# A decoder layer: the sliding-window branch's projection of half 0 by Strassen-Winograd blocks, with sums read out of open PSUM banks

## The chip, the cores and the metric

One program runs on one of the eight cores of a Trainium2 chip. The core has a matrix engine (TensorE, PE), three engines for elementwise work (VectorE or DVE, ScalarE or ACT, GpSimd or POOL), and a queue (SP) that issues the transfers between HBM and the on-chip memory SBUF. The matrix engine writes into PSUM, eight banks of 128 x 512 float32. The metric is the device time of one execution in microseconds, less being better; a kernel's time is the median of its runs.

## The reference

A layer over 2048 tokens with 1024 features, batch 1, depth 1. Two attention branches run side by side, are projected to the model width, gated, added, projected again and added to the residual:

```
proj = rms_norm(h, norm_gain) @ w_in          # 1024 -> 6400 columns, split in ten parts
o_sb = stick_breaking_attention(...)          # 8 heads of 64:  512 columns
o_sw = sliding_window_sink_attention(...)     # 16 query heads: 1024 columns
y_sb = (o_sb * silu(sb_z)) @ w_branch_sb
y_sw = (o_sw * silu(sw_z)) @ w_branch_swa     # 1024 x 1024: the product that is changed
merged = sigmoid(g_sb) * y_sb + sigmoid(g_sw) * y_sw
out = rms_norm(h + merged @ w_out, final_norm_gain)
```

All of it is float32. The kernel works with rounded operands and corrections: each matrix is split into a rounded high part `h` and the remainder `l`, and a product is the three products h h, h l and l h, so that a 128 x 128 by 128 x 512 block costs three matmuls.

## The kernel before

Tokens stand in four groups of 512. The program runs over them in two halves, `halves = ([2, 3], [0, 1])`: half 0 is groups 2 and 3, half 1 groups 0 and 1. For each half it computes the input projections, the sliding-window attention and the stick-breaking attention, with gate projections woven in to keep the matrix engine busy; intermediate results go to HBM (`ow` and `od`: outputs of the two attentions; `zw`, `zs`, `gw`, `gs`: gates that have their silu or sigmoid already). After both halves' attention comes `finish`, first for half 0, then for half 1.

`finish` for one half does three things. First the banded branch (the sliding window's): for each of eight tiles of 128 output columns `d` and both groups `g`, `project` runs 8 x 3 = 24 matmuls of 128 x 512 over the split outputs `osw[k, g]` and the split weights of tile `d` into one of six PSUM banks (tags g, z, t in turn), and DVE multiplies the bank by the gate `gw[d][g]` into `part[d, g]` (L286). Second the stick-breaking branch: 12 matmuls per tile and group over `osb`, gated and added to `part` (L296, L297), split into `merged` (L299, L300). Third the output projection with `w_out` and the norm (L336 to L357).

The right-hand operands are made by `gated`: load attention output and gate, multiply on DVE (L217), round on ACT into a buffer (L219), subtract on DVE for the remainder (L220). Those of half 0's banded branch (16 blocks, 32 buffers `ringl` in the pool of `rings`) are made while the last five gate tiles of half 1 run: the loop over `gts[rest:]` at the end makes up to four after each. A gate tile is two products of 24 matmuls (L464), each evacuated by a sigmoid on ACT (L615) and, for the silu gates, a multiply on DVE (L617) and a store to `zs`; they use the two banks of tag g, so DVE's multiply frees the bank for the product after the next. The stick-breaking operands `osb` are made in `finish`, after the third tile `d`, with load buffers of tag `a` (`AB = 6` of them).

The weights come through `weights`: load 512 KB into one of two buffers `raw`, round into `wh` and subtract into `wl` (three buffers each), on POOL in half 0's finish (L117, L123: four subtracts of 128 x 256). In half 0 the split pair is also stored to HBM (`kept`), and half 1 loads the pairs from there.

Each engine works through its own queue. PE's order is the program's; the orders of DVE, ACT, POOL and of the transfers on SP in this part are set by a scheduler at build time, which goes by its own estimate of times. `finish` opens its pool `wb` on the right-hand side of SBUF, where the pools of the gates' inputs (`x`) and of temporaries (`tmp`) are closed just before; `wb` holds `fg` (the final gain), 40 buffers `ringr`, six `a`, three `res` of 128 x 1024 and three `gt` for gates.

Of the kernel before, what the change touches and what calls it, by code (L numbers as in the profile page):

```python
# [7 lines left out]
F32 = mybir.dt.float32  # L8
F32R = mybir.dt.float32r
# [34 lines left out]
def f32(ap):  # L44
    return ap.bitcast(F32)
# [3 lines left out]
def tile_kernel(ctx, tc, x, xt, meta, metat, gain, w_in, w_sb, w_sw, w_out, sinks, fgain,  # L49
# [8 lines left out]
    def DMA(dst, src):  # L58
        nc.sync.dma_start(*(t.bitcast(F32) if t.dtype == F32R else t for t in (dst, src)))
# [34 lines left out]
    def dram(name, shape, dt=F32):  # L94
        return dp.tile(shape, dt, tag=name, name=name)
# [79 lines left out]
        DMA(raw, w[c0 // P])  # L175
        return raw

    def weights(c0, w=w_in, raw=None, split=split):

        if c0 in ready:  # L180
            return ready.pop(c0)
        n = w.shape[2]
        wh, wl = (wp.tile([P, KT, P], F32R, tag=t, name=t, bufs=3)[:, :n, :] for t in ("wh", "wl"))
        key = w.name, c0
        if key in kept:
            for t, k in zip((wh, wl), kept[key]):
# [14 lines left out]

    def rings():
        lp = cst.enter_context(tc.tile_pool(name="cl", bufs=1, side="left"))
        return lambda dt=F32R: lp.tile([P, GT], dt, tag="L", name="ringl", bufs=32)

    def gated(src, zz, k, g, ring, stg):

# [24 lines left out]
        V.tensor_tensor(l, t, f32(h), op=ALU.subtract)  # L232
        return h, l

    def finish(ringl, osw, first):
        cp = cst.enter_context(tc.tile_pool(name="wb", bufs=1, side="right"))
        banks = iter(range(1 << 30))

# [23 lines left out]
        for half, groups in enumerate(halves):  # L262
            part, merged, wo = {}, {}, {}

            def out_weights(k, ch):
                raw = small("a", AB)
                DMA(raw, w_out[0, k * P:(k + 1) * P, ch * GT:(ch + 1) * GT])
                h, l = wo[k, ch] = ringr(), ringr()
                A.copy(h, raw)
                V.tensor_tensor(l, raw, f32(h), op=ALU.subtract)  # L270

            osw2 = {}
            ws_of = {}
            order = [(d, g) for ds in ([0, 1, 2], *([d] for d in range(3, 8))) for g in groups for d in ds]
            for d, g in order:
                if d == 3 and g == groups[0]:
                    osb = {(k, g): gated(od, zs, k, g, ringr, lambda: small("a", AB)) for g in groups for k in range(4)}
                if d not in ws_of:
                    ws_of[d] = first if half == d == 0 else weights(d * P, w_sw)
                ws = ws_of[d]  # L280
                acc = bank()
                project(acc, ws, [osw[k, g] for k in range(8)])
                gt = small("gt", 3)
                DMA(gt, gw[d][g])
                part[d, g] = ringr(F32)
                V.tensor_tensor(part[d, g], acc, gt, op=ALU.mult)  # L286
# [1064 lines left out]
    for half, groups in enumerate(halves):  # L1351
# [100 lines left out]
            mid.close()  # L1452
        else:
            ringl = rings()
            osw = {}
# [64 lines left out]
```

## Time and profile before

| | |
|---|---|
| time, median of 3 runs | 2091.56 us (2090.66 to 2092.18) |
| the profiled execution | 2093.26 us, its span 2091.4 us |
| PE busy | 2076.3 us, 99% of the span |
| DVE, ACT, POOL busy | 70%, 52%, 17% |
| TensorE clock granted, mean | 0.999 |
| half 0's finish begins | 1647.60 us after the span's start |

A page of the profile gives busy time by engine, the span in forty slices, DMA queues, the chain that ended last, and groups of instructions. A row of a group reads: source line, engine, operation, output tile <- input tiles, shape and count, then busy time, mean ns of one, and the engine's idle time just before them with what ended it. A row of a timeline reads: start and duration in us, engine, line, operation, tiles, count, and in brackets idle time before it with what ended it. Matmul records overlap, as one starts before its predecessor is through; the distance between starts is what one costs.

### The profile page before, as it was taken

How to read it: one execution, taken by the hardware profiler on the slowest of the kernel's cores; microseconds unless marked ns; L12 is line 12 of the kernel's file. 1: busy time of each engine (PE TensorE's matmuls, PEld its weight loads, DVE VectorE, ACT ScalarE, POOL GpSimd, SP SyncE). 2: the span in 40 equal slices, each digit the busy share in tenths (PEclk: the TensorE clock that was granted, in tenths of full speed). 3: DMA queues.
4: the chain of work that ended last, by engine and by line, in shares of the span. 5: the costliest groups of instructions: out<-in, count | busy, mean ns of one | idle time of the engine just before them, and what ended most of it. 6: DMA issues, size and time to landing. Idle time of an engine off the chain costs nothing. (4 is left out here: it accounts for less than half of the span.)

```text
span 2091.4 us, 30949 instructions
## 1 busy us (share of the span) xinstructions
PE 2076.3 (99%) x10579; PEld 1744.8 (83%) x10579; DVE 1463.0 (70%) x2383; ACT 1091.4 (52%) x2657; POOL 345.7 (17%) x682
## 2 busy tenths in 40 slices
PE   9999999999999999999999999999999999999998
PEld 7888888888888888888888888888888888788887
DVE  7897986877687754887728788777774547464543
ACT  6677774577665335777735555655653212321121
POOL 1233444331000000233310000000000343000000
PEclk9999999999999999999999999999999999999999
DMA  9855555866377574435455344343424987568532
GB/s 338 307 195 201 188 175 179 252 199 185 91 278 298 209 247 163 159 126 177 150 171 161 120 130 129 114 129 98 121 83 165 350 318 223 182 229 305 154 100 91
DMA packets 170093, 391.46 MB, mean 187 GB/s; under 512 B 23728, under 2 KB 28208, under 8 KB 169936
## 3 DMA queue, kind: packets, MB, share of 16 engines
q1 hardware_dynamic: 169648, 389.23, 55.8%
q8 instruction: 83, 1.36, 0.3%
q14 instruction: 74, 0.61, 0.1%
q10 hardware_dynamic: 288, 0.27, 0.0%
HBM read 241.68 MB, written 145.18 MB: 185 GB/s over the span
## 5 line engine op out<-in xcount | busy, mean ns | idle before, releaser
L464 PE MATMUL ps_g<-xh,wh 128*128 128x512 f32 x1264 | 517.0, 409 | 1.1 <-DVE tmp L680 0.6
L464 PE MATMUL ps_g<-xl,wh 128*128 128x512 f32 x1264 | 495.6, 392 | 0.7 <-DVE xl L1199 0.6
L464 PE MATMUL ps_g<-xh,wl 128*128 128x512 f32 x1264 | 495.7, 392 | 0.0
L928 DVE TENSOR_TENSOR_SCAN row<-row 128x512 f32<-128x512 f32 (+4 forms) x256 | 290.1, 1134 | 116.2 <-POOL row L923 60.1
L464 PEld LDWEIGHTS ps_g<-xh,wl 128*128 128x128 f32 x1264 | 237.8, 188 | 52.7
L464 PEld LDWEIGHTS ps_g<-xh,wh 128*128 128x128 f32 x1264 | 238.5, 189 | 39.9 <-ACT xh L1198 1.4
L464 PEld LDWEIGHTS ps_g<-xl,wh 128*128 128x128 f32 x1264 | 239.2, 189 | 38.0 <-DVE xl L1199 1.8
L921 ACT ACTIVATE row<-ps_z 128x512 f32<-128x512 f32 (+4 forms) x352 | 175.1, 509 | 159.3 <-PE ps_z L918 155.0
L126 ACT ACTIVATE wth<-ps_t 128x512 fp32r<-128x512 f32 (+1 forms) x320 | 171.6, 536 | 61.4 <-PE ps_t L943 59.6
L127 DVE SCALAR_TENSOR_TENSOR wtl<-ps_t,wth 128x512 fp32r<-128x512 f32 (+1 forms) x320 | 188.7, 590 | 21.3 <-ACT wth L126 20.7
L918 PE MATMUL ps_z<-kt,q 128*128 128x512 f32 (+4 forms) x704 | 183.7, 349 | 2.0 <-ACT row L921 1.9
L943 PE MATMUL ps_t<-ident,row 128*128 128x128 f32 x1088 | 171.4, 273 | 1.0 <-DVE wtl L127 0.9
L943 PEld LDWEIGHTS ps_t<-ident,row 128*128 128x128 f32 x1088 | 134.5, 140 | 33.1 <-DVE wtl L127 1.8
L918 PEld LDWEIGHTS ps_z<-kt,q 128*128 128x128 f32 x704 | 124.4, 188 | 27.4 <-ACT row L921 5.1
L975 PE MATMUL ps_o<-wth,vc 128*128 128x512 f32 (+1 forms) x320 | 131.2, 410 | 0.0
L975 PE MATMUL ps_o<-wtl,vc 128*128 128x512 f32 (+1 forms) x320 | 116.4, 364 | 0.0
L767 ACT ACTIVATE sc<-sc,nm 128x129 f32<-128x129 f32 x256 | 100.0, 393 | 30.5 <-DVE nm L765 29.5
L934 POOL COPY mr<-row 128x16 f32<-128x16 f32 x128 | 28.4, 224 | 444.2 <-DVE row L928 401.8
L615 ACT ACTIVATE tmp<-ps_g 128x512 f32<-128x512 f32 x80 | 48.0, 600 | 80.5 <-PE ps_g L464 74.3
L299 ACT CAST ringl<-gt 128x512 fp32r<-128x512 f32 x32 | 19.9, 621 | 127.1 <-DVE gt L297 93.3
L117 POOL TENSOR_SCALAR wh<-raw 128x1024 fp32r<-128x1024 f32 (+1 forms) x45 | 49.8, 1108 | 212.7 <-PE ps_g L464 90.3
L123 POOL TENSOR_TENSOR wl<-raw,wh 128x256 fp32r<-128x256 f32 x88 | 83.2, 975 | 2.0
(442 smaller groups left out, 4202.3 us busy)
## 6 DMA issues: line engine op xcount, KB each, us to landing
wh<-h_in_w_in SPq DMA_DIRECT2D x66, 512.0 KB, 3.9
wl<-l_in_w_in SPq DMA_DIRECT2D x66, 512.0 KB, 5.1
h_in_w_in<-wh SPq DMA_DIRECT2D x50, 512.0 KB, 3.3
l_in_w_in<-wl SPq DMA_DIRECT2D x50, 512.0 KB, 4.1
raw<-in_w_in SPq DMA_DIRECT2D x49, 512.0 KB, 5.3
q<-qd SPq DMA_DIRECT2D x128, 128.0 KB, 3.2
vc<-vd SPq DMA_DIRECT2D x48, 256.0 KB, 3.2
kd<-tmp SPq DMA_DIRECT2D x32, 256.0 KB, 3.4
```

The costliest lines, as they stand in the source:

```text
L117: G.tensor_scalar(h, src, 1.0, 1.0, op0=ALU.mult, op1=ALU.mult)
L123: G.tensor_tensor(l[:, c], src[:, c], f32(h[:, c]), op=ALU.subtract)
L126: A.activation(h, acc, AF.Copy, scale=scale)
L127: V.scalar_tensor_tensor(l, acc, scale, f32(h), op0=ALU.mult, op1=ALU.subtract)
L464: T.matmul(acc, lhsT=a[:, k, :], rhs=b[:, k, :], start=k == i == 0, stop=k == KT - 1 and i == 2)
L615: A.activation(e, acc, AF.Sigmoid)
L767: A.activation(sc[:, hh, :], sc[:, hh, :], AF.Exp, bias=nm[:, hh:hh + 1], accum_out=den[:, hh:hh + 1])
L918: T.matmul(z[:, :m], lhsT=qt[:, j * P:(j + 1) * P], rhs=kt[h][:, k0 + c:k0 + c + m], start=t == 0, stop=t == 1)
L921: A.activation(r[:, c:c + m], z[:, :m], AF.Sigmoid, scale=-1.0)
L928: V.tensor_tensor_scan(r[:, :w], r[:, :w], r[:, :w], last[j] if n else 1.0, op0=ALU.mult, op1=ALU.min)
L943: T.transpose(tr[:, j * P:(j + 1) * P], rows_of[h, g, n - (j > i), j][:, k0:k0 + P], ident)
L975: T.matmul(o[:, :n], lhsT=v, rhs=r, start=first and r is wh, stop=last)
```

## The change

Half 0's banded product is done for pairs of column tiles. With the left and right operands cut in two along the inner dimension (k of 0 to 3 and 4 to 7, `HK = 4`), two tiles `d`, `d + 1` and the two groups `ga`, `gb` make a 2 x 2 by 2 x 2 block product, and seven block products of 12 matmuls take the place of eight. Four pairs make the eight tiles; `branch_by_pairs` does two pairs (`a`, `a + 1` and `b`, `b + 1`) at a time, for c = 0 and c = 4.

The right-hand blocks b11, b21, t1, b22, t2, t3, t4 (each for four k, high and low) are made by `outputs_blocks` in the gate tail for k = 0, 1, 2; for k = 3 only b11 and b21 are made there, and `last_blocks` makes the rest at the start of `finish`. `ringl` has 43 buffers instead of 32, `ringr` 29 instead of 40, and the constants' buffers `wm` and `vm`, no longer needed, serve as three more. The left-hand blocks come from `weight_blocks`, a generator of seven `wh`, `wl` tiles per c, each of two 512-column blocks: plain quarters are rounded on ACT with the subtract on POOL, the sums r1 to r4 and q1 to q4 are made on POOL (eight subtracts of 128 x 256 for each set, in buffers `a`), rounded on ACT, with the subtract on DVE. Two tiles are made ahead of `finish`; two whole quarters per c are loaded into buffers `res`.

Sums over products are formed in PSUM as far as they can be: the products for `za` (b11, then t2, then t3, then t4) go into one bank of tag o that stays open, and between them the partial sum is read: by `keep` (a copy on ACT to SBUF) or by `gated_sum` (on DVE: bank plus a kept partial sum, then times the gate). The last t4 product of each c is put off (`rest`) to after the first product that follows. `half_way`, after the b21 products of c = 4, makes the stick-breaking operands `osb` in buffers that are free by then. Half 0's weights are no longer stored; half 1 loads the plain weights again and splits them, with the rounding on ACT (`hsplit`) and the subtract on POOL.

```diff
@@ -175,7 +175,7 @@
         DMA(raw, w[c0 // P])
         return raw
 
-    def weights(c0, w=w_in, raw=None, split=split):
+    def weights(c0, w=w_in, raw=None, split=split, keep=True):
 
         if c0 in ready:
             return ready.pop(c0)
@@ -188,6 +188,8 @@
             return wh, wl
         raw = load(c0, w) if raw is None else raw
         split(wh, wl, raw)
+        if not keep:
+            return wh, wl
         kept[key] = [dram(f"{t}_{w.name}_{c0}", [P, n, P], F32R) for t in "hl"]
         for t, k in zip((wh, wl), kept[key]):
             if put_off is None:
@@ -201,7 +203,7 @@
 
     def rings():
         lp = cst.enter_context(tc.tile_pool(name="cl", bufs=1, side="left"))
-        return lambda dt=F32R: lp.tile([P, GT], dt, tag="L", name="ringl", bufs=32)
+        return lambda dt=F32R: lp.tile([P, GT], dt, tag="L", name="ringl", bufs=43)
 
     def gated(src, zz, k, g, ring, stg):
 
@@ -232,7 +234,205 @@
         V.tensor_tensor(l, t, f32(h), op=ALU.subtract)
         return h, l
 
-    def finish(ringl, osw, first):
+    def part_split(h, l, t):
+        A.copy(h, t)
+        V.tensor_tensor(l, t, f32(h), op=ALU.subtract)
+
...
+    def outputs_blocks(blk, k, ga, gb, ring, stg, zed):
+
+        def product(kk, g):
+            a, z = stg(), zed()
+            DMA(a, ow[kk][g])
+            DMA(z, zw[kk][g])
+            V.tensor_tensor(a, a, z, op=ALU.mult)
+            return a
+
+        def put(name, t):
+            h, l = blk[name, k] = ring(), ring()
+            part_split(h, l, t)
+
+        b11, b21 = product(k, ga), product(k + HK, ga)
+        put("b11", b11)
+        put("b21", b21)
+        if k == HK - 1:
+            return
+        b12, b22 = product(k, gb), product(k + HK, gb)
+        t3 = stg()
+        V.tensor_tensor(t3, b22, b12, op=ALU.subtract)
+        V.tensor_tensor(b12, b12, b11, op=ALU.subtract)
+        put("t1", b12)
+        put("b22", b22)
+        V.tensor_tensor(b22, b22, b12, op=ALU.subtract)
+        put("t2", b22)
+        put("t3", t3)
+        V.tensor_tensor(b21, b21, b22, op=ALU.subtract)
+        put("t4", b21)
+
+    def last_blocks(blk, ga, gb, ring, stg, zed):
+
+        k = HK - 1
+
...
+        for t, kk in ((b12, k), (b22, k + HK)):
+            z = zed()
+            DMA(t, ow[kk][gb])
+            DMA(z, zw[kk][gb])
+            V.tensor_tensor(t, t, z, op=ALU.mult)
+        t3, t4 = stg(), stg()
+        V.tensor_tensor(t3, b22, b12, op=ALU.subtract)
+        for part in blk["b11", k]:
+            V.tensor_tensor(b12, b12, f32(part), op=ALU.subtract)
+        put("t1", b12)
+        put("b22", b22)
+        V.tensor_tensor(b22, b22, b12, op=ALU.subtract)
+        put("t2", b22)
+        put("t3", t3)
+        for part, t in zip(blk["b21", k], (b22, None)):
+            if t is not None:
+                V.tensor_tensor(t4, f32(part), t, op=ALU.subtract)
+            else:
+                V.tensor_tensor(t4, t4, f32(part), op=ALU.add)
+        put("t4", t4)
+
+    def weight_blocks(spare_raw, sums):
+
+        def tile_of(*srcs):
+            wh, wl = (wp.tile([P, KT, P], F32R, tag=t, name=t, bufs=3) for t in ("wh", "wl"))
+            out = []
+            for i, (src, on_pool) in enumerate(srcs):
+                c = slice(i * HK, (i + 1) * HK)
+                A.copy(wh[:, c], src)
+                if on_pool:
+                    for j in range(0, HK, 2):
+                        G.tensor_tensor(wl[:, c][:, j:j + 2], src[:, j:j + 2], f32(wh[:, c][:, j:j + 2]), op=ALU.subtract)
+                else:
+                    V.tensor_tensor(wl[:, c], src, f32(wh[:, c]), op=ALU.subtract)
+                out.append((wh[:, c], wl[:, c]))
+            return out
+
+        def quarter(d):
+            raw = spare_raw()
+            DMA(raw, w_sw[d])
+            return raw[:, :HK], raw[:, HK:]
+
...
+        def combine(c, d):
+            (a11, a12), (a21, a22) = c, d
+            r1, r2, r3, r4 = (sums() for _ in range(4))
+            difference(r1, a21, a22, ALU.add)
+            difference(r2, r1, a11)
+            difference(r4, a12, r2)
+            difference(r3, a11, a21)
+            return r1, r2, r3, r4
+
+        for c in (0, 4):
+            one, two = ((raw[:, :HK], raw[:, HK:]) for raw in (load(d * P, w_sw) for d in (c, c + 2)))
+            yield tile_of((one[0], True), (two[0], True))
+            yield tile_of((one[1], True), (two[1], True))
+            low = quarter(c + 1)
+            r1, r2, r3, r4 = combine(one, low)
+            yield tile_of((r1, False), (r2, False))
+            yield tile_of((r4, False), (r3, False))
+            low2 = quarter(c + 3)
+            q1, q2, q3, q4 = combine(two, low2)
+            yield tile_of((q1, False), (low[1], True))
+            yield tile_of((q2, False), (q4, False))
+            yield tile_of((q3, False), (low2[1], True))
+
...
+        def product(acc, w, name, start=False, stop=False):
+            wh, wl = w
+            for k in range(HK):
+                h, l = blk[name, k]
+                T.matmul(acc, lhsT=wh[:, k, :], rhs=h, start=start and k == 0, stop=False, skip_group_check=True)
+                T.matmul(acc, lhsT=wh[:, k, :], rhs=l, start=False, stop=False, skip_group_check=True)
+                T.matmul(acc, lhsT=wl[:, k, :], rhs=h, start=False, stop=stop and k == HK - 1, skip_group_check=True)
+
+        def keep(d, g, acc):
+            t = part[d, g] = new()
+            A.copy(t, acc)
+
+        def gated_sum(d, g, acc):
+            t = part[d, g]
+            V.tensor_tensor(t, acc, t, op=ALU.add)
+            V.tensor_tensor(t, t, gate_of(d, g), op=ALU.mult)
+
...
+        rest = []
+        for c in (0, 4):
+            a, b = c, c + 2
+            w = fetch()
+            za = ps("o")
+            product(za, w[0], "b11", True)
+            keep(a, ga, za)
+            for f in rest:
+                f()
+            rest = []
+            zb = ps("o")
+            product(zb, w[1], "b11", True)
+            keep(b, ga, zb)
+            w = fetch()
+            for d, wi in zip((a, b), w):
+                acc = bank()
+                product(acc, wi, "b21", True, True)
+                gated_sum(d, ga, acc)
+            if c:
+                half_way()
+            w = fetch()
+            x = bank()
+            product(x, w[0], "t1", True)
+            keep(a + 1, gb, x)
+            product(za, w[1], "t2")
+            keep(a, gb, za)
+            w = fetch()
+            product(x, w[0], "b22", stop=True)
+            gated_sum(a, gb, x)
+            product(za, w[1], "t3")
+            gated_sum(a + 1, gb, za)
+            w = fetch()
+            x = bank()
+            product(x, w[0], "t1", True)
+            keep(b + 1, gb, x)
+
+            def close(d, z, w):
+                product(z, w, "t4", stop=True)
+                t = part[d, ga] = new()
+                V.tensor_tensor(t, z, gate_of(d, ga), op=ALU.mult)
+
+            close(a + 1, za, w[1])
+            w = fetch()
+            product(zb, w[0], "t2")
+            keep(b, gb, zb)
+            product(x, w[1], "b22", stop=True)
+            gated_sum(b, gb, x)
+            w = fetch()
+            product(zb, w[0], "t3")
+            gated_sum(b + 1, gb, zb)
+            rest.append(lambda d=b + 1, z=zb, w=w[1]: close(d, z, w))
+        return rest
+
+    def finish(ringl, blk, blocks, ahead, raws):
         cp = cst.enter_context(tc.tile_pool(name="wb", bufs=1, side="right"))
         banks = iter(range(1 << 30))
 
@@ -240,7 +440,7 @@
             return ps("gzt"[next(banks) % 3])
 
         def ringr(dt=F32R):
-            return cp.tile([P, GT], dt, tag="R", name="ringr", bufs=40)
+            return cp.tile([P, GT], dt, tag="R", name="ringr", bufs=29)
 
         def small(tag, bufs):
             return cp.tile([P, GT], F32, tag=tag, name=tag, bufs=bufs)
@@ -265,18 +465,43 @@
             def out_weights(k, ch):
                 raw = small("a", AB)
                 DMA(raw, w_out[0, k * P:(k + 1) * P, ch * GT:(ch + 1) * GT])
-                h, l = wo[k, ch] = ringr(), ringr()
+                if half == 0:
+                    rings_of = (ringr, ringr) if (k, ch) < (6, 1) or ch == 0 else (ringr, ringl) if k == 6 else (ringl, ringl)
+                else:
+                    rings_of = (ringl, ringl) if ch == 0 and k < 3 else (ringr, ringr)
+                h, l = wo[k, ch] = [ring() for ring in rings_of]
...
             osw2 = {}
             ws_of = {}
-            order = [(d, g) for ds in ([0, 1, 2], *([d] for d in range(3, 8))) for g in groups for d in ds]
+            rest = []
+            if half == 0:
+                osb = {}
+                spare_raw = lambda: cp.tile([P, D], F32, tag="xr", name="res", bufs=3).rearrange("p (k c) -> p k c", k=KT)
+                raws.append(spare_raw)
+                raws.append(lambda: small("a", AB).rearrange("p (k c) -> p k c", k=HK))
+
+                def gate_of(d, g):
+                    gt = small("gt", 3)
+                    DMA(gt, gw[d][g])
+                    return gt
+
+                def half_way():
+                    ring = slots([ringl() for _ in range(10)] + [ringr() for _ in range(3)] + [wm[0], wm[1], columns(vm[:, 0:2])])
+                    osb.update({(k, g): gated(od, zs, k, g, ring, lambda: small("a", AB)) for g in groups for k in range(4)})
+
+                last_blocks(blk, *groups, ringr, lambda: ringr(F32), lambda: small("a", AB))
+                rest = branch_by_pairs(groups, blk, ahead, blocks, part, bank, lambda: ringr(F32), gate_of, half_way)
+            else:
+                hsplit[0] = True
+            order = [(d, g) for ds in ([0, 1, 2], *([d] for d in range(3, 8))) for g in groups for d in ds] if half else ()
             for d, g in order:
                 if d == 3 and g == groups[0]:
-                    osb = {(k, g): gated(od, zs, k, g, ringr, lambda: small("a", AB)) for g in groups for k in range(4)}
+                    osb = {(k, g): gated(od, zs, k, g, ringl if k == 3 else ringr, lambda: small("a", AB))
+                           for g in groups for k in range(4)}
                 if d not in ws_of:
-                    ws_of[d] = first if half == d == 0 else weights(d * P, w_sw)
+                    ws_of[d] = weights(d * P, w_sw, keep=False)
                 ws = ws_of[d]
                 acc = bank()
                 project(acc, ws, [osw[k, g] for k in range(8)])
@@ -291,6 +516,9 @@
                 for g in groups:
                     acc = bank()
                     project(acc, ws, [osb[k, g] for k in range(4)])
+                    for f in rest:
+                        f()
+                    rest = []
                     gt = small("gt", 3)
                     DMA(gt, gs[d][g])
                     V.tensor_tensor(gt, acc, gt, op=ALU.mult)
@@ -1452,8 +1680,8 @@
             mid.close()
...
-            todo = [(k, g) for g in halves[0] for k in range(8)]
+            blk = {}
+            todo = list(range(HK))
...
-                for k, g in todo[:4]:
-                    osw[k, g] = gated(ow, zw, k, g, ringl, tmp)
-                del todo[:4]
-            for k, g in todo:
-                osw[k, g] = gated(ow, zw, k, g, ringl, tmp)
-    first = weights(0, w_sw)
+                for k in todo[:1]:
+                    ring = ringl if k < HK - 1 else slots([ringl(), wm[0], wm[1], columns(vm[:, 0:2])])
+                    outputs_blocks(blk, k, *halves[0], ring, tmp, ring_x)
+                del todo[:1]
+            assert not todo
+    raws = []
+    blocks = weight_blocks(lambda: raws[0](), lambda: raws[1]())
+    ahead = [next(blocks), next(blocks)]
     fst.close()
-    finish(ringl, osw, first)
+    finish(ringl, blk, blocks, ahead, raws)
     cst.close()
 
 _OUT = (2048, 1024)
```

More of the change, by code (lines that the diff above doesn't have):

```diff
@@ L233, in gated_in_place, with slots, columns @@
         return h, l
-    def finish(ringl, osw, first):
+    def part_split(h, l, t):
+        A.copy(h, t)
+        V.tensor_tensor(l, t, f32(h), op=ALU.subtract)
+    def slots(tiles):
+        it = iter(tiles)
+        return lambda: next(it)
+    def columns(t):
+        return t.rearrange("p a b c -> p (a b c)")
+    def outputs_blocks(blk, k, ga, gb, ring, stg, zed):
[24 more added lines that the diff above has]
+        put("t4", b21)
@@ new lines, in last_blocks, with put @@
+    def last_blocks(blk, ga, gb, ring, stg, zed):
+        k = HK - 1
+        def put(name, t):
+            h, l = blk[name, k] = ring(), ring()
+            part_split(h, l, t)
+        b12, b22 = stg(), stg()
+        for t, kk in ((b12, k), (b22, k + HK)):
[18 more added lines that the diff above has]
+        put("t4", t4)
@@ new lines, in weight_blocks, with difference @@
+    def weight_blocks(spare_raw, sums):
[16 more added lines that the diff above has]
+            return raw[:, :HK], raw[:, HK:]
+        def difference(t, a, b, op=ALU.subtract):
+            for j in range(0, HK, 2):
+                G.tensor_tensor(t[:, j:j + 2], a[:, j:j + 2], b[:, j:j + 2], op=op)
+            return t
+        def combine(c, d):
[19 more added lines that the diff above has]
+            yield tile_of((q3, False), (low2[1], True))
@@ new lines, in branch_by_pairs, with fetch @@
+    def branch_by_pairs(groups, blk, ahead, blocks, part, bank, new, gate_of, half_way):
+        ga, gb = groups
+        def product(acc, w, name, start=False, stop=False):
[12 more added lines that the diff above has]
+            V.tensor_tensor(t, t, gate_of(d, g), op=ALU.mult)
+        def fetch():
+            ahead.append(next(blocks, None))
+            return ahead.pop(0)
+        rest = []
[48 more added lines that the diff above has]
+        return rest
@@ L1454, in tile_kernel @@
             ringl = rings()
-            osw = {}
-            todo = [(k, g) for g in halves[0] for k in range(8)]
+            blk = {}
+            todo = list(range(HK))
             for mk in gts[rest:]:
```

## The prediction

> **What bounds the kernel now.** I read the page first, for the engine that is full; then the waits of TensorE over the last 590 us, where the change lies; then busy time by stretches of 50 us around half 0's finish; then the timelines of the engines and of the DMA queue from 1604 to 1706 us.
>
> ```profile
> span 2091.4 us, 30949 instructions
> PE 2076.3 (99%) x10579; PEld 1744.8 (83%) x10579; DVE 1463.0 (70%) x2383; ACT 1091.4 (52%) x2657; POOL 345.7 (17%) x682
> PE   9999999999999999999999999999999999999998
> ...
> PE ps_z L337 <- DVE ringr L270: 0.5, 2, 0.2
> ```
>
> The last line is the only wait of TensorE after 1500 us: 0.5 us in all. So every matmul taken out is worth its issue time, and every wait put in is paid in full: there is no slack on PE to hide it in.
>
> ```profile
> core 0: us, PE busy (x) PEld busy (x) DVE busy (x) ACT busy (x) POOL busy (x), PEclk, DMA share, GB/s
> ...
> 1600.00:1650.00 50.00, 50.00 (x222) 41.41 (x221) 27.96 (x38) 13.50 (x23) 12.26 (x12) 1.00 0.87 308
> 1650.00:1700.00 50.00, 50.00 (x223) 41.38 (x222) 24.38 (x30) 6.76 (x10) 22.31 (x24) 1.00 1.00 377
> 1700.00:1750.00 50.00, 50.00 (x222) 41.42 (x221) 24.04 (x32) 6.44 (x11) 16.47 (x20) 1.00 0.66 214
> ...
> 1647.60 0.39 PE L258 MATMUL ps_g<-ringl,wh 128*128 128x512 f32 x1
> 1653.04 0.39 PE L258 MATMUL ps_z<-ringl,wh 128*128 128x512 f32 x1
> ```
>
> Half 0's finish starts at 1647.60, called T0 below. From its first matmul to the next product's are 24 matmuls in 5.44 us, so one costs 0.2267 us of PE, not the 0.39 us of its own row, which overlaps its neighbours. The DMA engines are full (share 1.00, 377 GB/s) just there, while the vector engines are about half idle.
>
> **What the change removes.** The banded product of half 0 was 8 tiles x 2 groups x 24 = 384 matmuls; now it is 4 pairs x 7 products x 12 = 336. The program as built has 48 matmuls fewer on PE. 48 x 0.2267 = **-10.9 us**. Also gone are the 8 x 2 stores of split weights, 512 KB each, and half 1 loads 8 x 512 KB instead of 16 x 512 KB. That relieves a DMA system which PE does not wait for, so I cost it at nothing, as I do half 1's new splits: one cast and four POOL subtracts (4.5 us at most, rows below) per tile of 10.9 us of PE, with three buffers. If that cover went, PE would wait up to 3 us there.
>
> **What it adds and where it lies.** The sums of the right-hand blocks and of the weight quarters are new work for DVE, ACT and POOL, and its prices are in these rows:
>
> ```profile
> 1661.63 0.69 DVE L286 TENSOR_TENSOR ringr<-ps_g,gt 128x512 f32<-128x512 f32 x1 [8.28 <-DMA gt<-gw]
> 1662.24 0.68 DVE L286 TENSOR_TENSOR ringr<-ps_z,gt 128x512 f32<-128x512 f32 x1
> ...
> 1681.05 2.31 DVE L220 TENSOR_TENSOR ringr<-a,ringr 128x512 fp32r<-128x512 f32 x2
> 1683.28 1.22 DVE L217 TENSOR_TENSOR a<-a 128x512 f32<-128x512 f32 x1
> 1684.43 2.37 DVE L220 TENSOR_TENSOR ringr<-a,ringr 128x512 fp32r<-128x512 f32 x2
> ...
> 1670.53 2.83 POOL L123 TENSOR_TENSOR wl<-raw,wh 128x256 fp32r<-128x256 f32 x4
> 1681.76 4.49 POOL L123 TENSOR_TENSOR wl<-raw,wh 128x256 fp32r<-128x256 f32 x4
> L219 ACT CAST ringl<-tmp 128x512 fp32r<-128x512 f32 x16 | 9.9, 622 | 28.2 <-DVE tmp L217 28.1
> ```
>
> A 128x512 DVE operation costs 0.61 us of its queue alone (start to start, first two rows), and a 128x256 POOL subtract 2.83/4 = 0.71 us. Where POOL subtracts and DVE's SBUF-to-SBUF operations run together (1681 to 1686) both slow down: DVE five in 5.75 us, 1.15 us each, POOL 4.49/4 = 1.12 us. A cast on ACT is 0.62 us.
>
> Order matters as much as price. The engines take their queues in order:
>
> ```profile
> 1650.94 0.62 ACT L219 CAST ringl<-tmp 128x512 fp32r<-128x512 f32 x1 [2.58 <-DVE tmp L217]
> 1651.46 0.59 ACT L615 ACTIVATE tmp<-ps_g 128x512 f32<-128x512 f32 x1
> 1652.67 0.68 DVE L617 TENSOR_TENSOR tmp<-ps_g,tmp 128x512 f32<-128x512 f32 x1
> ```
>
> The sigmoid L615 reads the last gate product, ended by about T0+0.2; it ran 3.7 us later, behind a cast that stood waiting for DVE. Before, this hurt nobody. In the program as built, the copies `keep` (PSUM to SBUF, without which the next product may not go into the open bank) stand in the same ACT queue:
>
> ```
> ACT: cast wh<-r1, cast t1h, ... cast wh<-q1, cast t4h, keep(za), keep(zb), keep(x), ...
> ACT, second half: ... cast of gated output 7 of 8, keep(x), keep(za), ...
> ```
>
> (the gated outputs are the stick-breaking ones, which `half_way` queues). Terms in order of time, all waits of PE:
>
> **Gate tail: +1.5 (0 to 4).** DVE has 57 operations instead of 40 in the last four gate tiles (49 for the blocks, 8 silu products that release PE's two `ps_g` banks): 57 x 0.61 = 35 us of 43.5, with POOL beside 8 of them. Before, the L617 at 1652.67 came 5 us after its product; one product lasts 5.44 us, so there was hardly margin, and some of it goes.
>
> **t1 waits for its weights: +6 (4 to 9).** Buffers of the finish lie where the gates' inputs and temporaries were, so its loads cannot start before the gates end:
>
> ```profile
> 1653.37 0.32 SPq L59 DMA_DIRECT2D zs<-tmp  x1
> ...
> 1655.57 0.33 SPq L59 DMA_DIRECT2D fg<-in_fgain  x1
> 1655.96 1.53 SPq L59 DMA_DIRECT2D gt<-gw  x3
> ...
> raw<-in_w_sw SPq DMA_DIRECT2D x8, 512.0 KB, 6.4
> gt<-gs SPq DMA_DIRECT2D x32, 256.0 KB, 3.1
> ```
>
> fg goes 2.2 us after the last gate's store; the first gt, issued 0.4 us later, is used at 1661.63, 5.7 us after issue. Before, nothing urgent hung on that (a drained bank is needed 10.9 us later at the earliest, three rotate). Now the last store goes at about T0+1.8 (product drained 0.2, sigmoid 0.59, multiply 0.68, handing on), fg at 4.0, then at 0.4 us each two pairs for `last_blocks`, landing from 10.6, and the first quarter of weights, issued at 6.1, landing 6.4 later at 12.5. Two POOL sums (1.4 to 2.2) and a cast give r1 at 14.6 to 15.4, its low part 1.15 us later. PE reaches t1 after 48 matmuls, at 10.9. That is 4 to 6 us late; if the gate tail ends as late as before, 4 us more.
>
> **t2 waits for keep(za): +11.5 (3 to 13).** keep(za) stands behind the cast of t4h, which ends `last_blocks`. DVE's queue from its first product to that point holds 17 operations (12 of `last_blocks`, 5 low parts of weights), all SBUF to SBUF, and POOL has some 16 subtracts in the same stretch: 17 x 1.15 = 19.6 from 10.6, so 30.2, with two casts 31.5. t2 could start at 10.9+6+2.7 = 19.6. At 0.61 us each, 22.3. I take the crowded price, since POOL has no pause there.
>
> **Rest of the first four columns: +2 (0 to 3)**, for low parts a POOL operation late.
>
> **b22 of the second half waits for keep(x): +12 (8 to 19).** That copy stands behind the seventh of eight gated outputs. Their 24 loads share six `a` buffers, also used by the weight sums; the second to seventh find room only when the third tile of the second half is split, after product 15: 15 x 2.72 + 19.5 = T0+60.3. Before, the eight took
>
> ```profile
> 1664.19 0.69 DVE L213 TENSOR_TENSOR a<-a 128x512 f32<-128x512 f32 x1 [1.27 <-DMA a<-od]
> ...
> 1704.31 1.16 DVE L220 TENSOR_TENSOR ringr<-a,ringr 128x512 fp32r<-128x512 f32 x1 [0.69 <-ACT ringr L219]
> ```
>
> 41.3 us, 5.2 each, with DMA full. With 3.1 to 5.2 us for a landing (rows above) and 2.7 us of arithmetic, two in flight, one takes 3 to 4; I take 4: 60.3+24 = 84.3, plus the copy, 85. PE stands there at 73.9. At 3.5 the wait is 8, at 5.2 it is 19. Behind it POOL's remaining sums are late too: **+2.5 (0 to 4)**.
>
> **The clock: +3.5 (0 to 5).**
>
> ```profile
> 10.00:12.00 2.00, 1.86 (x5) 1.48 (x6) 2.00 (x5) 1.92 (x3) 0.00 (x0) 0.60 1.07 357
> 12.00:14.00 2.00, 2.00 (x7) 1.57 (x6) 1.90 (x4) 1.15 (x3) 0.00 (x0) 0.55 1.17 286
> ...
> 10.14 0.59 PE L464 MATMUL ps_g<-xl,wh 128*128 128x512 f32 x1 [0.62 <-DVE xl L1199]
> 10.53 0.63 PE L464 MATMUL ps_g<-xh,wh 128*128 128x512 f32 x1
> ...
> 13.89 0.39 PE L464 MATMUL ps_g<-xl,wh 128*128 128x512 f32 x1
> ```
>
> At the start, after a wait of 0.6 us, the granted clock was 0.60 and 0.55 for nearly 4 us: nine matmuls, from 10.14 to 13.89, took 3.75 us, not 9 x 0.2267 = 2.04, and 1.7 us were lost. Of the three long waits the first's slow stretch falls into the second wait; two count, 3.5 us. The Trainium skill ("TensorE: Matmul & The Clock Gate", Part 1) speaks against this change here: an idle window of about 3.4 us halves the clock until a busy window has passed; without that rule nothing in this trace says that a wait in mid-kernel is followed by slow matmuls, and the sum would be 3.5 us lower.
>
> The skill's page "SBUF — State Buffer" (Who interferes with whom) calls the port that VectorE and GpSimd share an exclusive lock. The rows say otherwise in size: a pair takes about 1.14 us, less than 0.61 + 0.71 = 1.32. By a full lock the 17 operations would take 22.4 us and the sum would be 2.8 us higher.
>
> **Sum.** 1.5 + 6 + 11.5 + 2 + 12 + 2.5 + 3.5 = 39 us of waits, less 10.9: +28.1. The profiled execution took 2093.26 us (span 2091.4), 1.7 above the median; it becomes 2121.4, and the median of 2091.56 becomes **2119.7 us**. 0.2%, 4.2 us, is about what a measurement of this kernel can tell from no change.
>
> **Rivals.**
> *The gain stands (faster).* If loads land in 3.1 us instead of 5.7 to 6.4 and POOL and DVE do not slow each other, t1's wait is 1 to 2, t2's 3 or less, and the outputs are done before b22. It decides where all waits stay under 6.7 us: then 2081 to 2087. For it: 12 MB less DMA traffic. Against: the contended rows and the queue order, which no faster load changes. 4%, and 3% for a tie near 2092.
> *Only the first half stalls.* If the outputs run at 3 us each or are loaded sooner, terms 12, 2.5 and one clock loss go: +28.1 - 16.3 = +12, 2104. 10%.
> *The outputs go at the old pace and the gate tail is late.* 3 + 9 + 13 + 3 + 19 + 4 + 5 - 10.9 = +45, 2137. For it: 5.2 us each is what was measured; against: the stores that filled the DMA are gone. 11%.
> That the matmuls are not saved is excluded by the program.
>
> **Numbers.** The forecast has 72%. Below 2104 lie the first rival, the tie and half of the second (12%), above 2134 most of the third (8 to 10%). Slower 93%, same 3%, faster 4%.
>
> **Right or wrong.** PE would show waits for ACT at the matmuls of `product` (t1: 4 to 7 us; t2: about 11, on the copy of `ps_o`; one of about 12 in the second half, on the copy of `ps_g`), ACT idle behind DVE ahead of the t4h cast, POOL subtracts near 1.1 us, and PEclk under 1 between T0 and T0+110. Wrong would be: no such waits, copies that run ahead of the casts, or half 1's finish changed by more than 3 us.

## The result, and the profile after

The changed kernel takes **2118.6 us** (median of 4 runs, 2117.56 to 2121.04), the kernel before 2091.87 beside it (4 runs, 2090.66 to 2092.55): ratio **1.0133**, 95% interval 1.0121 to 1.0144, 26.7 us slower. The forecast was 2119.7, slower. The profiled execution of after took 2121.04 us.

The head of its page:

```profile
span 2119.3 us, 31014 instructions
PE 2072.7 (98%) x10531; PEld 1738.3 (82%) x10531; DVE 1503.4 (71%) x2441; ACT 1126.0 (53%) x2717; POOL 392.1 (19%) x730
...
PE   9999999999999999999999999999999779999998
```

PE has 10531 instructions where it had 10579: the 48 matmuls are gone. In exchange two slices fall to 7 where PE had 9 throughout. The waits of TensorE after 1500 us (in total, times, longest):

```profile
PE ps_g L365 <- ACT ringr L371: 11.6, 1, 11.6
PE ps_o L365 <- ACT ringr L371: 9.0, 1, 9.0
PE ps_t L365 <- ACT wh L315: 5.1, 1, 5.1
PE ps_t L564 <- ACT ringr L473: 2.9, 1, 2.9
PE ps_g L692 <- DVE tmp L845: 1.9, 1, 1.9
PE ps_o L365 <- DVE ringr L421: 0.8, 1, 0.8
PE ps_o L365 <- DVE ringr L375: 0.7, 1, 0.7
```

In order of time these are the gate tail (1.9), t1 (5.1), t2 (9.0), the drain of `ps_o` between the halves (0.8), b22 of the second half (11.6), a late sum (0.7) and half 0's output projection (2.9). Before, there were 0.5 us of such waits. The timelines of VectorE, ScalarE and TensorE around the three long ones:

```profile
1663.41 0.62 ACT L315 CAST wh<-a 128x512 fp32r<-128x512 f32 x1 [13.34 <-POOL a L331]
1664.08 0.79 PE L365 MATMUL ps_t<-ringl,wh 128*128 128x512 f32 x1 [5.12 <-ACT wh L315]
...
1676.56 1.21 DVE L305 TENSOR_TENSOR ringr<-ringr,vm 128x512 f32<-128x512 f32 x1
1677.80 0.62 ACT L238 CAST ringr<-ringr 128x512 fp32r<-128x512 f32 x1 [5.22 <-DVE ringr L305]
1678.32 1.07 ACT L371 COPY ringr<-ps_o 128x512 f32<-128x512 f32 x2
1678.95 0.79 PE L365 MATMUL ps_o<-ringl,wh 128*128 128x512 f32 x1 [8.97 <-ACT ringr L371]
...
1733.77 0.62 ACT L221 CAST ringr<-a 128x512 fp32r<-128x512 f32 x1 [2.08 <-DVE a L219]
1734.29 0.58 ACT L371 COPY ringr<-ps_g 128x512 f32<-128x512 f32 x1
1734.93 0.80 PE L365 MATMUL ps_g<-ringl,wh 128*128 128x512 f32 x1 [11.65 <-ACT ringr L371]
```

T0 is the first matmul of half 0's finish, 1647.92 here. ACT stands still for the addition that ends the arithmetic of t4 in `last_blocks` (L305), casts t4h (the high part of t4), then copies the bank whose product ended at T0+2.7, and t2 starts 0.6 us later. In the second half the copy follows a gated output's cast (L221) in the same way. After each long wait the clock is low, by the windows (behind POOL's column stand PEclk, DMA share and GB/s):

```profile
1664.00:1668.00 4.00, 3.87 (x8) 2.67 (x9) 3.94 (x4) 1.59 (x4) 4.00 (x5) 0.50 0.11 43
1679.00:1683.00 4.00, 4.00 (x10) 3.13 (x11) 3.55 (x5) 0.87 (x2) 4.00 (x5) 0.50 0.15 21
1683.00:1687.00 4.00, 4.00 (x18) 3.31 (x17) 1.81 (x3) 1.63 (x3) 3.37 (x6) 0.93 0.69 245
1733.00:1737.00 4.00, 2.07 (x5) 1.69 (x6) 3.84 (x5) 2.21 (x4) 3.91 (x4) 0.50 0.34 88
```

After t1's and t2's waits eight to ten matmuls start in 4 us, where 18 fit; b22 begins in the middle of the last window, five matmuls in 2 us. From T0 to the end of the span after takes 471.4 us, before took 443.8 (2091.4 less 1647.60). This stretch leaves out what varies between executions upstream and is used below.

### The profile page after: what moved, and what is told of

It is laid out like the page before. It is cut to its first block, busy times and chain, and to the rows that moved or that the text cites. A ratio compares the mean times of both kernels' runs of the same rounds, so it can differ in the third digit from the quotient of the medians.

```text
span 2119.3 us, 31014 instructions
## 1 busy us (share of the span) xinstructions
PE 2072.7 (98%) x10531; PEld 1738.3 (82%) x10531; DVE 1503.4 (71%) x2441; ACT 1126.0 (53%) x2717; POOL 392.1 (19%) x730
## 5 line engine op out<-in xcount | busy, mean ns | idle before, releaser
L1027 POOL TENSOR_SCALAR_AFFINE_SELECT pm<-ph 64x256 fp32r<-64x256 f32 x128 | 63.3, 495 | 113.4 <-ACT ph L126 109.2
L576 ACT ACTIVATE sq<-res 128x512 bf16<-128x512 f32 (+1 forms) x33 | 20.4, 618 | 117.9 <-DVE res L568 117.8
```

## The experiments

Theory 1 is the prediction's reading: the order of ScalarE's queue holds the copies back. Theory 2, formed on the trace of after: DVE and POOL have more work between T0+10 and t4 than time, and while both subtract in SBUF each is slow, so whatever is moved ahead makes something else late. All times are medians.

### 1. The copies first

```
 product(zb, w[1], "b11", True); keep(b, ga, zb)
+if not c:
+    last_blocks(...)                # was ahead of the branch
+    ahead.append(next(blocks))      # the first sums: were ahead of za
```

> Edit: the last row of right-hand blocks (last_blocks) and the first sums are queued behind the first two keep copies, so keep(za) stands behind nothing of last_blocks; no work is added or taken out. Theory 1, the order of ScalarE's queue (the prediction's step): t2's wait of 9.0 us, with its 2.3 us of slow clock, goes; 2107 to 2110 us. Theory 2, the amount of work: the blocks and weights of the first half need some 17 VectorE operations at 1.15 us beside GpSimd's sums from about 10 us after the start of half 0's finish, in whatever order; the copy runs early, TensorE waits for last_blocks' blocks inside t1 instead (about 8 us, at its fourth row of blocks), and more for the b22 and later products; 2117 to 2121 us.

**2120.51 us**, ratio to before 1.0141 (1.0126 to 1.0156): nothing won. Its waits:

```profile
PE ps_g L365 <- ACT ringr L371: 11.6, 1, 11.6
PE ps_t L365 <- ACT ringr L238: 6.5, 1, 6.5
PE ps_t L365 <- ACT wh L315: 2.8, 1, 2.8
PE ps_t L365 <- ACT ringr L371: 2.8, 1, 2.8
...
PE ps_t L366 <- DVE ringr L239: 0.8, 1, 0.8
```

The copy now runs at T0+4.1, and t2 does not wait. In its place t1 waits for its fourth row of blocks (the cast L238: 6.5, and 0.8 for the low part), and b22 waits 2.8 for the copy of `x`, which stands behind the same t4h cast. Theory 1 as the prediction put it falls: the copy was only the last thing late. VectorE's timeline shows the rest:

```profile
1667.42 1.21 DVE L320 TENSOR_TENSOR wl<-a,wh 128x512 fp32r<-128x512 f32 x1
1668.55 1.21 DVE L295 TENSOR_TENSOR ringr<-ringr,wm 128x512 f32<-128x512 f32 x1
1669.68 1.21 DVE L320 TENSOR_TENSOR wl<-a,wh 128x512 fp32r<-128x512 f32 x1
1670.82 2.34 DVE L239 TENSOR_TENSOR ringr<-ringr 128x512 fp32r<-128x512 f32 x2
```

Every operation is at the crowded price, and the planner of the queues, which orders all but TensorE's by its own estimate, has put five low parts of weights (L320), most of them for later products, ahead of t1's low part (L239 at 1670.82). So this run moved more than the copies, and does not by itself tell work from order.

### 2. The weight quarters first

```
-DMA(fg, fgain...)                      # ahead of last_blocks' loads
+for d in (1, 3): DMA(spare_raw(), w_sw[d])
 ...
+DMA(fg, fgain...)                      # behind the branch
```

> Edit: the loads of the first two weight quarters go ahead of the load of fg and of last_blocks' loads (fg's load is moved behind the banded branch); no work is added or taken out. The prediction's step: t1 waits because its quarter is asked for at 6.1 to 7.6 us after the start of half 0's finish; asked for at 4, t1's wait of 5.1 us falls to 1 to 2 and the time by 3 to 4, 2114 to 2116 us, with the wait at t2 as it was. Rival, the amount of work: GpSimd's sums start 4 us sooner and so run beside more of last_blocks' work on VectorE, t1 starts sooner but waits some 8 us at its fourth row of blocks, and t2 8 us; the time stays at 2117 to 2120 us.

**2120.03 us**, ratio 1.0138 (1.0123 to 1.0154). The rival holds:

```profile
PE ps_g L368 <- ACT ringr L374: 11.2, 1, 11.2
PE ps_t L368 <- ACT ringr L238: 7.8, 1, 7.8
PE ps_o L368 <- ACT ringr L374: 7.4, 1, 7.4
```

t1's wait for weights is gone (0.3 left), and 7.8 us stand at its fourth row of blocks. The late load was the last cause of the 5.1 us and not the only one.

### 3. Without `last_blocks`

```
-last_blocks(...)
+for name in ("t1", "b22", "t2", "t3", "t4"): blk[name, 3] = blk[name, 2]
```

> Left out: the arithmetic and the loads of last_blocks; the products of row 3 take row 2's blocks instead. TensorE's work is the same. Theory 1 (queue order) and theory 2 (amount of work) both have t2's wait of 9.0 us gone and t1's down to 3 to 4, with 12 VectorE operations fewer beside GpSimd's sums: 2105 to 2109 us. Rival, late weights alone: t2 would wait for GpSimd's sums in any case (r2's and r4's splits), and the time would fall by under 4 us, 2115 to 2118. The second half's wait at b22 stays at 11 to 14 us in all.

**2103.39 us**, ratio 1.0057 (1.0040 to 1.0074): 15.2 less than after, somewhat more than expected. t2's wait is gone, t1's is 1.7, b22's is 11.4, as in after. Weights alone would have let t2 start in time.

### 4. Without the sums

```
-r1..r4 = sums of quarters on GpSimd
+return a21, a22, a11, a12
```

> Left out: the eight sums of weight quarters of each pair (GpSimd's L331 operations, 48 in all); raw quarters are split in their place, as many splits as before, and six buffers are free of sums. Theory 2 (amount of work at the port that VectorE and GpSimd share, and a buffers held by sums): last_blocks' operations run at 0.6 to 0.7 us instead of 1.15, t2's wait falls from 9.0 to 6 to 7, and the second half's gated outputs find free buffers at once, so that the wait at b22 falls from 11.7 to 1 to 3 us; 2099 to 2105 us. Theory 1 (order on ScalarE alone, outputs at 4 us each whatever the buffers): the wait at b22 stays at 9 to 12 and the time falls by 3 to 6 us, 2112 to 2116.

**2101.94 us**, ratio 1.0051 (1.0036 to 1.0066): 16.7 less than after.

```profile
PE ps_o L360 <- ACT ringr L366: 6.7, 1, 6.7
PE ps_t L360 <- ACT wh L315: 3.6, 1, 3.6
```

t2's wait is 6.7 as expected, and b22's 11.6 us are gone altogether, though the eight gated outputs are as many: the first of them begins at 1668.3 instead of 1693.6, since its loads find `a` buffers. The crowding goes with the sums too, but it is not what slowed the outputs in after, where GpSimd works 2.1 us between 1704 and 1733. There the second half's first four sums hold four of the six buffers. One load of an output goes out at 1698.24, the next only once the first low part made from a sum is through:

```profile
1709.23 1.28 DVE L320 TENSOR_TENSOR wl<-a,wh 128x512 fp32r<-128x512 f32 x2
1709.93 0.32 SPq L59 DMA_DIRECT2D a<-od  x1
```

So the outputs are late by the sums' buffers, as the prediction's step at b22 had it. They need not be the only cause: the queue stood 4.2 us for a gate's buffer (released by L421) just before it waited for L320. This run has 32 GpSimd instructions fewer than after (698 against 730), not the 48 that the expectation names.

### 5. All queues by hand

The same products, but every queue of the branch in the order of need:

```
+with tc.manual_schedule(engines={DVE, Activation, Pool, SP}):
+    quarter 1; b12, b22; quarter 3; gates    # loads
+    r1, r2 -> cast, low; t1; b22; t2; r4; r3; t3; q1; q2; t4; q4; q3
+    # sums of columns 0 to 3 on V, of 4 to 7 on G; keep before casts that wait
+    # gated outputs: two loaded in the first half, then one between products
+output weights' second half loaded ahead of half 1's raw weights; gt 3 -> 4 buffers
```

The low parts of four plain quarters, on GpSimd in after, are on VectorE too, here and in experiments 6 and 9.

> The same seven products, same arithmetic, with the order of all queues of half 0's banded branch written out by hand: the weight sums of columns 0 to 3 on VectorE instead of GpSimd (those of columns 4 to 7 stay on GpSimd, early), each sum, block and low part queued in the order in which TensorE needs it, each keep copy ahead of casts that wait, quarters loaded first, the gated outputs spread over the second half; the second column half of the output weights is loaded ahead of half 1's weights; four gt buffers instead of three (one ringr fewer). Theory 2 (amount of work at the shared port, and when it starts): VectorE alone needs 18 operations of 0.61 us for what t1 to t3 wait for, 11 us, where the crowded pairs took 17 x 1.15 us, so the waits of 5.1, 9.0 and 11.7 us shrink to 2 to 3 in the first half and 2 to 4 in the second, the wait of 2.9 at the output projection and the slow clock go: 2079 to 2086 us, faster than before. Rival: reading partial sums out of open banks, with a copy or an add between two products of a bank, costs its wait in any order; then 2092 or more.

**2087.43 us** (11 runs) against 2090.9 of before (27): ratio **0.9984**, interval 0.9975 to 0.9993, the fastest of all. It is 3.5 us under before and about 31 under after. It misses the expected range (2079 to 2086) by 1.4 us; the rival, 2092 or more, is 4.6 off. Page and waits:

```profile
span 2084.9 us, 30994 instructions
PE 2067.0 (99%) x10531; PEld 1735.0 (83%) x10531; DVE 1505.9 (72%) x2453; ACT 1126.4 (54%) x2717; POOL 374.4 (18%) x706
```
```profile
PE ps_g L1037 <- DVE tmp L1190: 1.8, 1, 1.8
PE ps_z L447 <- ACT ringr L453: 0.9, 1, 0.9
PE ps_g L807 <- ACT wm L539: 0.8, 1, 0.8
PE ps_g L808 <- DVE vm L540: 0.6, 1, 0.6
PE ps_t L448 <- DVE ringr L507: 0.2, 1, 0.2
```

As many matmuls as after, VectorE as busy as after (1505.9 against 1503.4), and 2.5 us of waits behind T0 instead of 30. So neither the open banks nor the amount of vector work as such costs the time. From T0 (1648.97) to the end it takes 435.9, which is 7.9 less than before: 10.9 less the waits, within 1 us. Between the two profiled executions that leaves 6.6 us (2093.26 less 2086.66), since T0 is 1.4 later, by the gate tail's wait of 1.8, which was left alone. The medians lie closer, 3.5: the profiled execution of before was 2.4 above the median here, that of this kernel 0.8 below its own.

### 6. By hand, with the sums on GpSimd

```
-r1 = a21 + a22 ...  (VectorE, columns 0 to 3, all eight sums)
+the same on GpSimd, two operations each
```

> As e5_by_hand, but the weight sums of columns 0 to 3 are on GpSimd, as in the kernel after; the order is otherwise the same. Theory 2: VectorE's operations beside them take 1.15 instead of 0.61 us again, and t1, t2 and b22 wait 8 to 9 us in all instead of 3: 4 to 7 us slower than e5_by_hand. Rival, only the order of the queues mattered: within 1.5 us of e5_by_hand.

**2092.41 us**, ratio 1.0009 (0.9999 to 1.0018): 5.0 above experiment 5, as theory 2 has it. VectorE's timeline there with GpSimd's beside it, then VectorE's in experiment 5 for the same work:

```profile
1659.11 1.21 DVE L496 TENSOR_TENSOR wl<-a,wh 128x512 fp32r<-128x512 f32 x1
1660.25 1.22 DVE L581 TENSOR_TENSOR a<-ringr,ringl 128x512 f32<-128x512 f32 x1
1659.74 2.32 POOL L484 TENSOR_TENSOR a<-raw,a 128x256 f32<-128x256 f32 x2
```
```profile
1659.82 0.68 DVE L496 TENSOR_TENSOR wl<-a,wh 128x512 fp32r<-128x512 f32 x1
1660.42 0.68 DVE L581 TENSOR_TENSOR a<-ringr,ringl 128x512 f32<-128x512 f32 x1
```

1.14 us from start to start beside GpSimd, 0.60 without. But this kernel has the sums of after on the engine of after, and is 26 us faster than after, of which 6.7 belong to the stage behind the branch (experiment 9). So theory 2 is wrong where it says "in whatever order": by these differences the order is worth some 19 us and the crowding 5, only it is the order of all queues, with early loads, and not that of two copies. The 19 include the four low parts that stay on VectorE here; what they give was not tried apart.

### 7. The waits filled

```
+fill(20)   # ahead of t1      fill(46) ahead of t2      fill(48) ahead of b22
```

> The kernel after, with matmuls that nobody reads put into the three long waits: 20 before t1, 46 before t2, 48 before b22 of the second half (into a free PSUM bank, from blocks that lie in SBUF anyway), 0.2267 us each, so 4.5, 10.4 and 10.9 us: TensorE is not idle for long. Theory: the idle time halves the granted clock, so t2's and b22's products run at 0.2267 us a matmul again, the clock before t2 makes no difference in time, and 2.3 + 1.6 us come back: 2113 to 2116 us. Rival: the low clock comes of something else (a cap on power, the copies): no change, 2117 to 2121; if the added matmuls delay the product behind them, up to 2 us slower.

**2119.57 us**, ratio 1.0139 (1.0125 to 1.0152): no gain in the median, where 2113 to 2116 was expected. Once more, beside after on the same chip:

> e7_filled_waits once more, beside the kernel after on the same chip (e11_after_again), to tell 2 us apart. Theory: the clock's two stretches cost 2.3 and 1.6 us, of which 1.5 come back as a longer wait behind b22, as the traces of e7_filled_waits and of after have it: 1.5 to 2.5 us under e11_after_again. Rival: none of it is left in the total, within 1 us.

> The kernel after, unchanged, for e10_filled_waits_again to stand against: 2117 to 2120 us by every theory.

Filled **2120.61** (2119.99 to 2121.26), after **2119.73** (2118.89 to 2120.23). The filled kernel's windows (the second run):

```profile
1679.00:1683.00 4.00, 3.56 (x15) 2.92 (x16) 4.00 (x5) 1.98 (x5) 4.00 (x5) 1.00 0.18 60
1733.00:1737.00 4.00, 3.94 (x17) 3.30 (x18) 4.00 (x5) 2.33 (x5) 4.00 (x4) 1.00 0.13 25
```

The clock stays at 1.00 where after has 0.50, so idle time is what lowers it. And from T0 to the end the filled kernel takes 469.5 and 469.6 us in its two profiles, after 471.4 and 471.6: in this stretch 2 us come back, as the second expectation had it, where the first had 3.9 (a wait for a sum behind b22, 0.5 to 0.7 us in after, is 2.2 here). The totals do not show it: T0 lies later in the second pair of profiles (1648.73 against 1646.86), not in the first (1647.52 against 1647.92). Where the total loses what the stretch wins stays open.

### 8. Half 1's part alone

```
 # in the kernel before
-store split weights in half 0, load them in half 1
+keep=False: half 1 loads raw weights and splits them, cast on ScalarE
```

> The kernel before with only the weights' part of the change: the split banded weights are not stored in half 0, and half 1 loads and splits them again (its cast on ScalarE, as after). The prediction's step put this at nothing, up to 3 us: 2091 to 2093. Against it, after waits 2.9 us at half 0's output projection for output weights whose loads stand on the DMA queue behind a load of half 1's raw weights: 2094 to 2097, with that wait in the trace.

**2093.26 us** (10 runs), ratio 1.0012 (1.0003 to 1.0021): 2.4 slower. The DMA queue's timeline, then the wait:

```profile
1783.01 0.33 SPq L59 DMA_DIRECT2D raw<-in_w_sw  x1
1783.39 7.41 SPq L59 DMA_DIRECT2D a<-in_w_out  x8
```
```profile
PE ps_z L340 <- ACT ringr L271: 2.0, 1, 2.0
```

The output weights' loads go out directly behind a load of half 1's raw weights on the same queue; after them ScalarE waits 5.3 us for the first to land. Counted from each kernel's T0 they go out 2.7 us later than in before (137.9 against 135.2). The median lies between the two expected ranges; the wait is there, 2.0 of the 2.9. No gain from the stores that are gone shows in the total.

### 9. Only the branch by hand

```
 # experiment 5 without its last line: gt 3 buffers, loads ordered as in after
```

> As e5_by_hand, but only the banded branch is ordered by hand: three gt buffers, 29 ringr, and the order of the output weights and of half 1's loads as in the kernel after. Theory 2 with the finding of e8_half1_alone: the branch itself waits as little as in e5_by_hand (4 to 5 us), but VectorE comes out of it behind, and with three gt buffers (each held for about 4 us of work and 4 of loading while a product lasts 2.72) it cannot catch up before half 0's output projection, where TensorE then waits for the last merged tiles and the output weights, 6 to 10 us: 2092 to 2097 us. Rival, the branch's order was all that mattered: within 3 us of e5_by_hand, 2086 to 2090.

**2094.16 us** (10 runs), ratio 1.0009 (1.0000 to 1.0018): 6.7 above experiment 5, or 6.2 when each is set against before as measured beside it (2091.39 here, 2090.9 there).

```profile
PE ps_g L905 <- DVE ringl L867: 2.4, 2, 2.1
...
PE ps_g L903 <- ACT ringl L866: 1.3, 1, 1.3
```

These two, 3.7 us, stand at the start of half 0's output projection, for the last merged tiles, and are less than the 6 to 10 us expected. The eight matmuls behind them, at a granted clock of 0.55 to 0.59, took another 1.7 us more than at full speed. The branch itself waits as in experiment 5, within 1 us. So what was done in the branch (its order, and the sums' engine) is worth 24 us of the 31, and the rest lies in the stage behind it, 40 us later. How much of that the fourth gt buffer gives and how much the order of the loads was not tried apart.

## Why the prediction was right

- **48 matmuls, -10.9:** held. Experiment 5 has the same 48 fewer and keeps 7.9 of it behind T0.
- **Gate tail, +1.5:** 1.9 in this profile, 0.9 in after's second one, 0.2 in experiment 1's. Held, in a size that varies.
- **t1, +6:** 5.1, for r1's cast behind POOL, as said; fg went at T0+4.05 (forecast 4.0). The size held. That the load is the cause held in part: with the load early (experiment 2) a wait of 7.8 stands at t1's fourth row instead.
- **t2, +11.5:** 9.0, and 2.4 us of slow matmuls in t1 that this wait would else have held: 11.4. VectorE does have 17 operations up to the cast of t4h, and they take 20.0 us (1657.80 to 1677.77, forecast 19.6). But the crowded price holds for twelve of them (1.14 us each); the first five ran at about 0.72, before GpSimd's sums, and then VectorE stood 2.2 us for the cast of r1. That the stretch came out right is in part luck. The step that failed is the reading that the copy's place in the queue is the cause: experiment 1 takes it away and wins nothing.
- **Rest of the first columns, +2:** 0.8, and not for a low part but for the drain of a bank (L421). **b22, +12:** 11.6, with the copy behind an output's cast, the outputs behind the `a` buffers (experiment 4). From the load at T0+62.0 to the seventh cast at T0+85.9 they take 4.0 us each, as forecast (60.3, 84.3); the working's own 85 less 73.9 is 11.1, not 12. **POOL's sums behind it, +2.5:** 0.7.
- **Half 1 at nothing:** wrong by 2 to 3 us. The step costed its loads and splits as work, and did not ask what stands behind those loads on SP; experiment 8 prices it at 2.4, and after waits 2.9 for it (1.4 in its second profile). Two waits sized too high, the rest of the first columns by 1.2 and POOL's sums by 1.8, made up for it, so that the nearness of the sum (28.1 against 26.7) is in part luck.
- **The clock, +3.5:** 2.3 at t2 (12 matmuls in 5.0 us instead of 2.7) and 1.6 at b22 by the trace, 3.9; but of that only 2 is price, since behind b22 the vector chain would have been late anyway (experiment 7). The clock rule that the prediction cited from the Trainium skill, "TensorE: Matmul & The Clock Gate", Part 1, agrees with the trace in kind: 0.50 after waits of 5 to 12 us, and 1.00 where the waits were filled. It was 0.50 after a wait of 2.8 us too (experiment 1, 1681 to 1683), which is shorter than the window of about 3.4 us that the prediction took from there.
- The page "SBUF — State Buffer" of the Trainium skill (Who interferes with whom) calls the port of VectorE and GpSimd an exclusive lock. Experiment 6 agrees with the prediction's rows in size: a 128x512 operation on VectorE and a 128x256 one on GpSimd each take 1.14 us side by side, less than the two prices alone together (0.60 and 0.71). Whether they share the port or take turns at it, these rows do not show.
- Of the rivals, "only the first half stalls" is what experiment 4 makes of the kernel; it was not what the outputs did, for they were slowed by buffers that the sums held.

## What to carry to other kernels

When TensorE has no slack, a product saved is worth its issue time only if every operand of the remaining ones is ready in the order of need; count what the other engines must finish before each product, at the crowded price, and write that order into all their queues. Moving the one instruction that the wait names mostly uncovers the next late one, so test with the work left out before believing an order. And a transfer that nobody waits for can still cost: ask what stands behind it on its queue.

## What was not expected of the hardware

- The slow clock cost less than its matmuls: 0.427 us each for 3 to 6 us after the three long waits, but where another engine is late at the same time that is cover. 114 matmuls that nobody reads kept the clock at 1.00 and left the total where it was (2120.61 against 2119.73).
- Two engines that subtract in SBUF slow each other to 1.14 us an operation (experiment 6); an addition that reads PSUM did not take part. In after, with GpSimd's two operations at 0.93 us each beside them:

```profile
1679.50 0.68 DVE L375 TENSOR_TENSOR ringr<-ps_g,ringr 128x512 f32<-128x512 f32 x1
1680.10 0.67 DVE L375 TENSOR_TENSOR ringr<-ps_z,ringr 128x512 f32<-128x512 f32 x1
```

0.60 us from start to start, the price of an operation alone.
